# Two layers of a streaming encoder on one core: recurrent gates as 64x128 blocks, their heads and the local attention heads in alternating row halves of the array

## The chip, the cores and the metric

The kernel runs on one core of one Trainium2 chip. The metric is the device time of one execution in microseconds (us), as the median of several runs. Engine names are those of the profile: PE is the matrix engine (TensorE), PEld its weight loads, DVE the vector engine, ACT the scalar engine, SP the engine that issues the loads of weights. A matmul multiplies a stationary operand, which a weight load brings into the 128x128 array, with a moving operand of N columns, and writes to PSUM.

## The reference

Two layers run over a sequence of 256 positions with 1024 features, in float32. Only the parts of the mixer that the change touches are shown; before and after the mixer each layer has a gated feed-forward block (width 2816).

```python
# recurrent branch: 16 heads of 64 features, two gates per head
xb = xc.reshape(B, S, LRU_BLOCKS, LRU_BLOCK)                 # 16 blocks of 64
r  = sigmoid(einsum('bshi,hij->bshj', xb, wa) + ba)
gi = sigmoid(einsum('bshi,hij->bshj', xb, wx) + bx)
log_a = -LRU_C * r * softplus(-lam);  a = exp(log_a)
b = sqrt(max(1 - exp(2 * log_a), 0)) * gi * xc               # then a scan over time
# local attention: 8 query heads and 2 key/value heads of 64, window of 3 chunks of 64
s = einsum('bcqkgd,bcskd->bckgqs', qb, kb) * 64 ** -0.5 - slopes * dist
p = softmax over keys, with a learned sink per head
o = einsum('bckgqs,bcskd->bcqkgd', p, vb)
```

A third branch is attention over 256 memory tokens. The three branches are projected, gated, summed and projected again.

## The kernel before, in words

Activations are kept feature-major: 128 features on the partitions, 256 positions along the free dimension, eight such chunks for 1024 features. Every weight is cut on the host into blocks of 128x128, in the order in which the kernel uses them, eight blocks to a slab of 128x1024 numbers. SP loads slabs; ACT rounds each to a high half (`whi`, line 194) and DVE subtracts to get the low half (`wlo`, line 195). A product is formed with reduced-precision matmuls: high weight times both halves of the activations (512 columns, line 219) and low weight times the high half (256 columns, line 220).

The order of the work is written out by hand. `block` hands out the next weight block; at the first block of each slab it prepares the slab that is three ahead and calls `tick`, which runs the side tasks that are due. `at(n, f)` makes f due n ticks later, so a tick comes once per 8 blocks, just before the matmuls of the next slab. What is issued so goes into the in-order queues of PE, ACT and DVE.

In `mix` (one call per layer) the stretch that matters runs as follows.

- `conv` projects the recurrent input and runs a convolution on ACT and DVE; its result is split into halves `xcs`.
- Then come the projections of keys and values (`pkv`), and four pairs of query projections (`pq`, `pq`, `pcq`, `pcq`), each of 16 blocks. After each of the four pairs stands `lru_gates(p)`: two gates times two chunks, each gate of a chunk being one 128x128 block with two 64x64 heads on its diagonal and zeros elsewhere, and three matmuls of 256 columns per block (lines 670 to 672, tile `lg`). Four sigmoids of 128x256 on ACT take them out of PSUM (lines 675 and 676), and DVE multiplies `gi` with the convolution (line 677).
- `decay(c)` puts three ACT functions (`e`, `nth`, `a`, lines 706 to 708) and one DVE operation (`ms`, line 709) per chunk on the ticks behind that, under the projections `pyr` and `pgt`. `e` and `nth` take turns in a pool of three buffers, so that `nth` of a chunk waits for `ms` of the chunk before.
- `attention_tasks` spreads the two attentions over the same ticks. For query tile qt (0 or 1) and key/value head g (0 or 1), `win_scores` runs four matmuls over 64 partitions (line 835, tile `ws`, the upper 64 partitions for g = 1), DVE adds the distance (line 837), `win_max`, `win_exp` and `win_norm` (line 861) make probabilities `P`, and `win_transpose` turns them on PE (line 877, tile `wt`) and has ACT copy them (line 878, `PT`). For qt = 1 the scores of a g are split over two ticks.

Two PSUM pools matter. `mm` has three tiles of two banks, used by all projections and by `lg`; `att` has two tiles of one bank, used in turn by `ws`, `wt` and the memory attention's `ms`. A full-precision matmul, as in `ws`, `wt` and `wv`, is recorded as two passes, transposes as one. `win_values` (lines 888 and 890, tile `wv`) writes g = 0 and g = 1 to different halves of the array's columns, one after the other.

`join` takes a projection out of PSUM: ACT copies one half, and one tick later DVE adds the other (line 261), which frees the `mm` tile; line 635 then multiplies with the norm.

Of the kernel before, what the change touches and what calls it, by code (L numbers as in the profile page):

```python
# [22 lines left out]
AF = mybir.ActivationFunctionType  # L23
ALU = mybir.AluOpType
# [10 lines left out]
HB = 8  # L35
EPS = 1e-6
BIG = 1e30
NBLK = 2 * 1728
NSLAB = NBLK // HB
WIN_SCALE = 0.125  # L40
MEM_SCALE = 128.0 ** -0.5
# [29 lines left out]
def cols(c):  # L71
    return slice(c, c + 128)
# [22 lines left out]
class Trunk:  # L95
# [46 lines left out]
    def mm(self, nm):  # L142
        return self.pmm.tile([128, 2, 2, 256], F32, tag="mm", name=self.name(nm))
# [481 lines left out]
    def mix(self, l, norm, nxt):  # L625
        nc, V, A, G = self.nc, self.nc.vector, self.nc.scalar, self.nc.gpsimd
        w = lambda base, p: (lambda m: [("w_in", l, cols(128 * k), cols(base + 128 * (2 * p + m))) for k in range(KT)])
# [4 lines left out]
        xcs = Halves(self, "xcs")  # L632
# [28 lines left out]
        gi, r = self.big("gi"), self.big("r")  # L661

        def lru_gates(p):
            ps = self.mm("lg")
            for i, nm in enumerate(("lru_wa", "lru_wx")):
                for m in range(2):
                    c = 2 * p + m
                    hi, lo = self.block(nm, l, None, ("bd", c))
                    mm = nc.tensor.matmul
                    mm(ps[:, i, m, :], hi, xcs.hi(c), start=True, stop=False)  # L670
                    mm(ps[:, i, m, :], hi, xcs.lo(c), start=False, stop=False)
                    mm(ps[:, i, m, :], lo, xcs.hi(c), start=False, stop=True)
            for m in range(2):
                c = 2 * p + m
                A.activation(r[:, c, :], ps[:, 0, m, :], AF.Sigmoid, bias=self.vec("lru_ba", l, c))
                A.activation(gi[:, c, :], ps[:, 1, m, :], AF.Sigmoid, bias=self.vec("lru_bx", l, c))
            V.tensor_tensor(gi[:, sl(p), :], gi[:, sl(p), :], xc[:, sl(p), :], op=ALU.mult)

        kv = self.ps2.tile([128, 2, 256], F32, tag="kv", name=self.name("kv"), bufs=1)
        ps = self.pair("pkv", w(C_K, 0), norm.xs)  # L680
# [10 lines left out]
        qcq = self.big("qcq")  # L691
        for p in range(4):
            if p < 2:
                ps = self.pair("pq", lambda m: [("w_in", l, cols(128 * k), ("q", 2 * p + m)) for k in range(KT)], norm.xs)
            else:
                ps = self.pair("pcq", w(C_CQ, p - 2), norm.xs)
            project(qcq[:, sl(p), :], ps)
            lru_gates(p)


        a, ms = self.big("a"), self.big("ms")
# [51 lines left out]
        for p in range(4):  # L753
            ps = self.pair("pyr", w(C_YR, p), norm.xs)
# [11 lines left out]
        for g in range(3):  # L766
            gt = self.big(f"g{g}")
            gates.append(gt)
            for p in range(4):
                ps = self.pair("pgt", w(C_G + 1024 * g, p), norm.xs)  # L770
# [32 lines left out]
        n = self.Norm(self, *nxt)  # L803
# [16 lines left out]
    def attention_tasks(self, l, kv, vt, qcq, out):  # L820
        nc, V, A, T, G = self.nc, self.nc.vector, self.nc.scalar, self.nc.tensor, self.nc.gpsimd
        k = kv[:, 0, :]
        sinks = self.vec("attn_sinks", l)
        st = {}

        def win_scores(qt, g, js):
            n = 128 * (qt + 1)
            qs = slice(128 * qt, 128 * qt + 128)
            gp = slice(64 * g, 64 * g + 64)
            P = self.h4("P") if js[0] == 0 else st["w", qt, g]  # L830
            st["w", qt, g] = P
            d = self.dist[:, 0:128] if qt == 0 else self.dist[:, 128:384]
            ps = self.att("ws").rearrange("p (a n) -> p a n", n=n)
            for j in js:
                T.matmul(ps[:, j - js[0], :], qcq[gp, j, qs], k[gp, 0:n], start=True, stop=True)
            for j in js:
                V.scalar_tensor_tensor(P[:, j, 0:n], d, -8.0 * 2.0 ** -(4 * g + j + 1), ps[:, j - js[0], :],
                                       op0=ALU.mult, op1=ALU.add)

        def win_max(qt, g):  # L840
            n = 128 * (qt + 1)
            P = st["w", qt, g]
            mx, ng, es, den = (self.sm(s) for s in ("mx", "ng", "es", "den"))
            sk = sinks[:, 4 * g:4 * g + 4]
            V.tensor_reduce(mx, P[:, :, 0:n], axis=AX.X, op=ALU.max)
            V.scalar_tensor_tensor(mx, mx, WIN_SCALE, sk, op0=ALU.mult, op1=ALU.max)
            V.tensor_scalar(ng, mx, -1.0, None, op0=ALU.mult)
            V.tensor_tensor(es, sk, mx, op=ALU.subtract)
            st["w", qt, g] = (P, ng, es, den)

        def win_exp(qt, g):
            n = 128 * (qt + 1)
            P, ng, es, den = st["w", qt, g]
            for j in range(4):
# [80 lines left out]
                             start=(t == 0), stop=(t == 1))  # L935
            self.split(ps, out["C"], 0, 4, delay=0)

        for (qt, g), ts in (((0, 0), (1, 3, 4, 7)), ((0, 1), (3, 5, 6, 9)), ((1, 0), (10, 12, 13, 15)),
                            ((1, 1), (13, 15, 16, 18))):
            for i in range(qt + 1):  # L940
                self.at(ts[0] + i, win_scores, qt, g, range(2 * i, 2 * i + 2) if qt else range(4))
            self.at(ts[0] + qt, win_max, qt, g)
            for t, f in zip(ts[1:], (win_exp, win_norm, win_transpose)):
                self.at(t, f, qt, g)
        for qt, ts in enumerate(((16, 17, 19, 22), (19, 20, 22, 24))):
# [6 lines left out]
    def run(self):  # L952
        nc = self.nc
        n = self.start()
        for l in range(DEPTH):
# [14 lines left out]
            if not last:  # L970
                n.then(5, 7)
        assert len(self.order) == NBLK

# [4 lines left out]
def pack_weights(order, inp):  # L978
    out = np.zeros((NSLAB, 128, HB, 128), np.float32)
    for i, (w, l, rows, cls) in enumerate(order):  # L980
        dst = out[i // HB, :, i % HB, :]
        if rows is None:
            c = cls[1]
            dst[0:64, 0:64] = inp[w][l, 2 * c]
            dst[64:128, 64:128] = inp[w][l, 2 * c + 1]
            continue
        if isinstance(rows, tuple):
            rows = QROWS[rows[1]]
        if isinstance(cls, tuple):
            cls = QROWS[cls[1]]  # L990
        dst[...] = inp[w][l][rows, cls]
    return out.reshape(NSLAB, 128, HB * 128)


def pack_vectors(inp):
    pk = np.zeros((128, NVEC), np.float32)
    for (v, l), o in VOFF.items():
        if v == "final_norm":
            a = inp[v].reshape(8, 128).T
        elif v == "attn_sinks":  # L1000
            a = np.broadcast_to(inp[v][l], (128, 8))
        else:
            a = inp[v][l].reshape(-1, 128).T
        pk[:, o:o + a.shape[1]] = a
    return pk

# [38 lines left out]
```

## Time and profile before

| | |
|---|---|
| median of 3 runs (1285.68 to 1287.1) | 1286.26 us |
| the profiled execution's own time | 1286.29 us |
| its span, first to last instruction | 1284.3 us |
| PE busy | 1269.7 us (99%) |
| PE weight loads busy | 1116.4 us (87%) |
| DVE busy | 980.7 us (76%) |
| ACT busy | 758.8 us (59%) |
| TensorE clock granted, mean share of full | 0.997 |

The profile has a page (busy times, the chain of work that ended last, the costliest groups) and a trace that can be asked for timelines and sums over stretches. A timeline line gives start, length, engine, source line, operation, the tile written and the tiles read, and in brackets the idle time before it and who ended it. Matmuls are pipelined, so their lengths overlap: what a matmul costs is the distance between starts.

### The profile page before, as it was taken

How to read it: one execution, taken by the hardware profiler on the slowest of the kernel's cores; microseconds unless marked ns; L12 is line 12 of the kernel's file. 1: busy time of each engine (PE TensorE's matmuls, PEld its weight loads, DVE VectorE, ACT ScalarE, POOL GpSimd, SP SyncE). 2: the span in 40 equal slices, each digit the busy share in tenths (PEclk: the TensorE clock that was granted, in tenths of full speed). 3: DMA queues.
4: the chain of work that ended last, by engine and by line, in shares of the span. 5: the costliest groups of instructions: out<-in, count | busy, mean ns of one | idle time of the engine just before them, and what ended most of it. 6: DMA issues, size and time to landing. Idle time of an engine off the chain costs nothing.

```text
span 1284.3 us, 19477 instructions
## 1 busy us (share of the span) xinstructions
PE 1269.7 (99%) x7514; PEld 1116.4 (87%) x7514; DVE 980.7 (76%) x1398; ACT 758.8 (59%) x1129; POOL 0.3 (0%) x5
## 2 busy tenths in 40 slices
PE   9999999999999999999999999999999999999997
PEld 7888898888888888888988888988888889888886
DVE  8788766888789887666668775669887898776754
ACT  6656544587578555554456564447857675655542
POOL 0000000000000000000000000000000000000000
PEclk9999999999999999999999999999999999999998
DMA  8665655555446555566556656555554465665651
GB/s 295 212 183 167 212 192 168 178 178 166 133 131 199 194 180 189 191 193 198 185 192 204 193 183 195 185 185 155 181 164 132 153 197 176 197 192 187 196 183 47
DMA packets 64748, 232.42 MB, mean 181 GB/s; under 512 B 7312, under 2 KB 7440, under 8 KB 64400
## 3 DMA queue, kind: packets, MB, share of 16 engines
q1 hardware_dynamic: 64224, 230.65, 56.3%
q8 instruction: 59, 0.97, 0.3%
q10 hardware_dynamic: 432, 0.53, 0.1%
q14 instruction: 33, 0.27, 0.1%
HBM read 230.10 MB, written 1.05 MB: 180 GB/s over the span
## 4 chain that ended last, share of the span: by engine, by line
PE 90%; DVE 5%; ACT 2%; issue 1%; DMA 1%; SPq 0%; DVEq 0%; ACTq 0%
PE pg L219 11%; PE pu L219 11%; PE pd L219 9%; PE pgt L219 6%; PE pu L220 6%; PE pg L220 6%; PE pd L220 5%; PE pbr L219 4%; PE pgt L220 3%; DVE wlo L195 2%; PE pyr L219 2%; PE pbr L220 2%; PE pxr L219 2%; PE pwo L219 2%; PE pgu L219 2%; PE pd L238 2%
## 5 line engine op out<-in xcount | busy, mean ns | idle before, releaser
L195 DVE TENSOR_TENSOR wlo<-st,whi 128x1024 fp32r<-128x1024 f32 (+2 forms) x438 | 524.6, 1206 | 252.9 <-ACT whi L194 252.8
L194 ACT ACTIVATE whi<-st 128x1024 fp32r<-128x1024 f32 (+2 forms) x438 | 444.1, 1045 | 35.9 <-PE pd L219 20.5
L219 PE MATMUL pg<-xs,whi 128*128 128x512 f32 x640 | 225.4, 394 | 0.0
L219 PE MATMUL pu<-xs,whi 128*128 128x512 f32 x640 | 225.2, 394 | 0.0
L219 PE MATMUL pd<-h,whi 128*128 128x512 f32 x528 | 184.1, 393 | 0.0
L220 PE MATMUL pg<-xs,wlo 128*128 128x256 f32 x640 | 179.4, 280 | 0.0
L220 PE MATMUL pu<-xs,wlo 128*128 128x256 f32 x640 | 179.3, 280 | 0.0
L220 PE MATMUL pd<-h,wlo 128*128 128x256 f32 x528 | 148.0, 280 | 0.0
L219 PEld LDWEIGHTS pg<-xs,whi 128*128 128x128 f32 x640 | 119.9, 187 | 27.2
L219 PEld LDWEIGHTS pu<-xs,whi 128*128 128x128 f32 x640 | 119.8, 187 | 27.0
L219 PE MATMUL pgt<-xs,whi 128*128 128x512 f32 x384 | 139.1, 405 | 0.0
L220 PEld LDWEIGHTS pu<-xs,wlo 128*128 128x128 f32 x640 | 121.0, 189 | 0.0
L220 PEld LDWEIGHTS pg<-xs,wlo 128*128 128x128 f32 x640 | 121.0, 189 | 0.0
L219 PEld LDWEIGHTS pd<-h,whi 128*128 128x128 f32 x528 | 98.9, 187 | 22.5
L220 PE MATMUL pgt<-xs,wlo 128*128 128x256 f32 x384 | 107.5, 280 | 0.0
L220 PEld LDWEIGHTS pd<-h,wlo 128*128 128x128 f32 x528 | 99.8, 189 | 0.0
L219 PEld LDWEIGHTS pgt<-xs,whi 128*128 128x128 f32 x384 | 72.1, 188 | 19.5 <-issue 3.0
L258 ACT COPY g<-pg 128x512 f32<-128x512 f32 x40 | 23.5, 586 | 100.5 <-PE pg L220 93.3
L220 PEld LDWEIGHTS pgt<-xs,wlo 128*128 128x128 f32 x384 | 72.5, 189 | 0.2
L270 ACT ACTIVATE h<-u 128x512 fp32r<-128x512 f32 x44 | 27.8, 632 | 46.0 <-DVE u L523 43.8
L320 ACT ACTIVATE xs<-x,pk 128x256 fp32r<-128x256 f32 x40 | 18.7, 504 | 60.8 <-DVE x L557 21.6
L238 PE MATMUL pd<-h,wlo 128*128 128x256 f32 x176 | 49.8, 283 | 0.0
(246 smaller groups left out, 2259.0 us busy)
## 6 DMA issues: line engine op xcount, KB each, us to landing
st<-wpack SPq DMA_DIRECT2D x428, 512.0 KB, 3.8
st<-wpack SPq DMA_DIRECT2D x8, 256.0 KB, 5.3
mem<-memT SPq DMA_DIRECT2D x2, 1024.0 KB, 6.5
x<-xT SPq DMA_DIRECT2D x4, 256.0 KB, 5.4
outT<-xg SPq DMA_DIRECT2D x2, 256.0 KB, 2.6
outT<-xg ACTq DMA_DIRECT2D x2, 256.0 KB, 2.8
cst<-cst SPq DMA_DIRECT2D x1, 320.0 KB, 6.1
pk<-pk SPq DMA_DIRECT2D x1, 128.0 KB, 5.8
```

Source lines behind the costliest of these rows:

```text
L194: nc.scalar.activation(hi[:, c], st[:, c], AF.Copy)
L195: nc.vector.tensor_tensor(lo[:, c], st[:, c], hi[:, c].bitcast(F32), op=ALU.subtract)
L219: mm(both, hi, X.both(k), start=(k == 0), stop=False)
L220: mm(out[:, 0, :], lo, X.hi(k), start=False, stop=(k == n - 1))
L238: mm(out, lo, X.hi(k), start=False, stop=(k == len(blocks) - 1))
L258: self.nc.scalar.copy(dst, ps[:, :, 1, :])
L270: hi = lambda: self.nc.scalar.activation(X.hi(k, n), src, AF.Copy)
L320: self.t.nc.scalar.activation(self.xs.hi(k), x[:, k, :], AF.Copy, scale=self.t.vec(self.v, self.l, k))
```

## The change

The gates' weights are packed without zeros. For chunk c with heads 2c and 2c+1 one block now holds in its upper 64 rows the two gates' 64x64 matrices of head 2c side by side, and in its lower 64 rows those of head 2c+1 in swapped order. A matmul takes 64 rows of the block and of the activations and writes 128 columns: both gates of one head. So a chunk needs one block where it needed two, and still six matmuls of 256 columns, now alternating between the upper and the lower rows. The two heads go to the two banks of the `lg` tile. Each sigmoid covers 64 partitions, and there are eight per pair of chunks instead of four. The biases of the second gate are stored with their halves swapped.

The scores of the local attention are taken for both g in one task, into both `att` tiles, with matmuls alternating between g = 0 and g = 1. For qt = 0 that is one task at tick 1 (before: ticks 1 and 3), for qt = 1 two tasks at ticks 10 and 11 (before: 10, 11, 13 and 14). The number of slabs falls by one per layer.

```diff
-NBLK = 2 * 1728
+NBLK = 2 * 1720
...
-            for i, nm in enumerate(("lru_wa", "lru_wx")):
-                for m in range(2):
-                    c = 2 * p + m
-                    hi, lo = self.block(nm, l, None, ("bd", c))
-                    mm = nc.tensor.matmul
-                    mm(ps[:, i, m, :], hi, xcs.hi(c), start=True, stop=False)
-                    mm(ps[:, i, m, :], hi, xcs.lo(c), start=False, stop=False)
-                    mm(ps[:, i, m, :], lo, xcs.hi(c), start=False, stop=True)
+            mm = nc.tensor.matmul
+            halves = (slice(0, 64), slice(64, 128))
             for m in range(2):
                 c = 2 * p + m
-                A.activation(r[:, c, :], ps[:, 0, m, :], AF.Sigmoid, bias=self.vec("lru_ba", l, c))
-                A.activation(gi[:, c, :], ps[:, 1, m, :], AF.Sigmoid, bias=self.vec("lru_bx", l, c))
+                hi, lo = self.block("lru_w", l, None, ("bd", c))
+                for i, (w, x) in enumerate(((hi, xcs.hi(c)), (hi, xcs.lo(c)), (lo, xcs.hi(c)))):
+                    for j, q in enumerate(halves):
+                        mm(ps[:, j, m, :], w[q, :], x[q, :], start=(i == 0), stop=(i == 2))
+            for m in range(2):
+                c = 2 * p + m
+                for j, q in enumerate(halves):
+                    A.activation(r[q, c, :], ps[q, j, m, :], AF.Sigmoid, bias=self.vec("lru_ba", l, c)[q, :])
+                    o = halves[1 - j]
+                    A.activation(gi[q, c, :], ps[o, j, m, :], AF.Sigmoid, bias=self.vec("lru_bx", l, c)[o, :])
...
+            ps = [self.att("ws").rearrange("p (a n) -> p a n", n=n) for _ in range(2)]
             for j in js:
-                T.matmul(ps[:, j - js[0], :], qcq[gp, j, qs], k[gp, 0:n], start=True, stop=True)
-            for j in js:
-                V.scalar_tensor_tensor(P[:, j, 0:n], d, -8.0 * 2.0 ** -(4 * g + j + 1), ps[:, j - js[0], :],
-                                       op0=ALU.mult, op1=ALU.add)
+                for g in range(2):
+                    gp = slice(64 * g, 64 * g + 64)
+                    T.matmul(ps[g][:, j - js[0], :], qcq[gp, j, qs], k[gp, 0:n], start=True, stop=True)
+            for g in range(2):
+                P = self.h4("P") if js[0] == 0 else st["w", qt, g]
+                st["w", qt, g] = P
+                for j in js:
+                    V.scalar_tensor_tensor(P[:, j, 0:n], d, -8.0 * 2.0 ** -(4 * g + j + 1), ps[g][:, j - js[0], :],
+                                           op0=ALU.mult, op1=ALU.add)
...
-        for (qt, g), ts in (((0, 0), (1, 3, 4, 7)), ((0, 1), (3, 5, 6, 9)), ((1, 0), (10, 12, 13, 15)),
+        self.at(1, win_scores, 0, range(4))
+        for i in range(2):
+            self.at(10 + i, win_scores, 1, range(2 * i, 2 * i + 2))
+        for (qt, g), ts in (((0, 0), (1, 3, 4, 7)), ((0, 1), (3, 5, 6, 9)), ((1, 0), (11, 12, 13, 15)),
                             ((1, 1), (13, 15, 16, 18))):
-            for i in range(qt + 1):
-                self.at(ts[0] + i, win_scores, qt, g, range(2 * i, 2 * i + 2) if qt else range(4))
-            self.at(ts[0] + qt, win_max, qt, g)
+            self.at(ts[0], win_max, qt, g)
```

How instructions stand on PE where the last group of gates meets the first scores, in layer 0 (names end in buffer numbers; `xcs` are the convolution's halves, `kv` and `qcq` keys and queries). Before:

```order
L670 MATMUL lg_2753<-xcs_2207,whi_2660 128x256
L671 MATMUL lg_2753<-xcs_2207,whi_2660 128x256
L672 MATMUL lg_2753<-xcs_2207,wlo_2661 128x256
L835 MATMUL ws_2784<-kv_2414,qcq_2474 128x128 x4
L219 MATMUL pyr_2774<-xs_1420,whi_2684 128x512 [waits DVE_49]
```

With the change:

```order
L672 MATMUL lg_2759<-xcs_2207,whi_2652 128x256 x4
L672 MATMUL lg_2759<-xcs_2207,wlo_2653 128x256 x2
L836 MATMUL ws_2793<-kv_2414,qcq_2474 128x128
L836 MATMUL ws_2794<-kv_2414,qcq_2474 128x128
L836 MATMUL ws_2793<-kv_2414,qcq_2474 128x128
L836 MATMUL ws_2794<-kv_2414,qcq_2474 128x128
L836 MATMUL ws_2793<-kv_2414,qcq_2474 128x128 [waits DVE_49]
L836 MATMUL ws_2794<-kv_2414,qcq_2474 128x128
L836 MATMUL ws_2793<-kv_2414,qcq_2474 128x128
L836 MATMUL ws_2794<-kv_2414,qcq_2474 128x128
L219 MATMUL pyr_2784<-xs_1420,whi_2676 128x512 [waits DVE_49]
```

The scores of both g now stand directly behind the gates, and the second visit, 16 blocks later, is gone.

On PE at tick 10, in the projection `pgt`, before:

```order
L220 MATMUL pgt_3077<-xs_1421,wlo_2978 128x256
L835 MATMUL ws_3115<-kv_2414,qcq_2474 128x256 [waits Activation_49]
L835 MATMUL ws_3115<-kv_2414,qcq_2474 128x256
L219 MATMUL pgt_3077<-xs_1420,whi_3010 128x512
L220 MATMUL pgt_3077<-xs_1420,wlo_3011 128x256 [waits DVE_49]
```

With the change:

```order
L220 MATMUL pgt_3087<-xs_1421,wlo_2988 128x256
L836 MATMUL ws_3124<-kv_2414,qcq_2474 128x256 [waits Activation_49]
L836 MATMUL ws_3125<-kv_2414,qcq_2474 128x256 [waits Activation_49]
L836 MATMUL ws_3124<-kv_2414,qcq_2474 128x256
L836 MATMUL ws_3125<-kv_2414,qcq_2474 128x256
L219 MATMUL pgt_3087<-xs_1420,whi_3020 128x512
L220 MATMUL pgt_3087<-xs_1420,wlo_3021 128x256 [waits DVE_49]
```

The visit now takes two `att` tiles where it took one, and each has its own wait for ACT.

On DVE behind the last gates, before:

```order
L837 SCALAR_TENSOR_TENSOR P_2783<-cst,ws_2784 128x128 [waits PE_49]
L837 SCALAR_TENSOR_TENSOR P_2783<-cst,ws_2784 128x128 x3
L845 TENSOR_REDUCE mx_2793<-P_2783 128x4 [waits DVE_49]
L846 SCALAR_TENSOR_TENSOR mx_2793<-mx_2793,pk 128x4 [waits DVE_49]
L847 TENSOR_SCALAR ng_2794<-mx_2793 128x4 [waits DVE_49]
L848 TENSOR_TENSOR es_2795<-pk,mx_2793 128x4
L709 SCALAR_TENSOR_TENSOR ms_2772<-e_351_2801,nth_2802 128x256 [waits Activation_49]
L195 TENSOR_TENSOR wlo_2826<-st_2682,whi_2825 128x1024 [waits DMAHW6_49,Activation_49]
L709 SCALAR_TENSOR_TENSOR ms_2772<-e_353_2829,nth_2830 128x256 [waits Activation_49]
L195 TENSOR_TENSOR wlo_2856<-st_2716,whi_2855 128x1024 [waits DMAHW7_49,PE_49,Activation_49]
L837 SCALAR_TENSOR_TENSOR P_2864<-cst,ws_2865 128x128 [waits PE_49]
L837 SCALAR_TENSOR_TENSOR P_2864<-cst,ws_2865 128x128 x3
```

With the change:

```order
L841 SCALAR_TENSOR_TENSOR P_2803<-cst,ws_2793 128x128 [waits PE_49]
L841 SCALAR_TENSOR_TENSOR P_2803<-cst,ws_2793 128x128 x3
L841 SCALAR_TENSOR_TENSOR P_2808<-cst,ws_2794 128x128 [waits PE_49]
L841 SCALAR_TENSOR_TENSOR P_2808<-cst,ws_2794 128x128 x3
L849 TENSOR_REDUCE mx_2813<-P_2803 128x4 [waits DVE_49]
L850 SCALAR_TENSOR_TENSOR mx_2813<-mx_2813,pk 128x4 [waits DVE_49]
L851 TENSOR_SCALAR ng_2814<-mx_2813 128x4 [waits DVE_49]
L852 TENSOR_TENSOR es_2815<-pk,mx_2813 128x4
L711 SCALAR_TENSOR_TENSOR ms_2782<-e_350_2821,nth_2822 128x256 [waits Activation_49]
```

The four operations of the second tile stand ahead of the first `ms`, the DVE part of `decay`, where they stood behind the second.

## Rows read from the trace of the kernel before

**Rows 1.** Page, busy time: us (share of the span) and instructions.
```profile
PE 1269.7 (99%) x7514; PEld 1116.4 (87%) x7514; DVE 980.7 (76%) x1398; ACT 758.8 (59%) x1129; POOL 0.3 (0%) x5
```
**Rows 2.** Page, the chain of work that ended last, by engine.
```profile
PE 90%; DVE 5%; ACT 2%; issue 1%; DMA 1%; SPq 0%; DVEq 0%; ACTq 0%
```
**Rows 3.** Sum over one stretch for tile lg: window, length, PE, PEld, ACT busy.
```profile
269.20:270.70 1.50, 1.45 (x12) 1.45 (x12) 0.00 (x0) 1.00 0.93 273
```
**Rows 4.** Timeline of PE, tick 10: start us, length us, engine, line.
```profile
306.25 0.28 PE L220 MATMUL pgt<-xs,wlo 128*128 128x256 f32 x1
306.45 1.13 PE L835 MATMUL ws<-kv,qcq 64*128 64x256 f32 x4
...
307.85 0.28 PE L220 MATMUL pgt<-xs,wlo 128*128 128x256 f32 x1
```
**Rows 5.** Timeline of PE, last gates, first scores and the projection behind them.
```profile
277.67 0.28 PE L672 MATMUL lg<-xcs,wlo 128*128 128x256 f32 x1
277.88 1.16 PE L835 MATMUL ws<-kv,qcq 64*128 64x128 f32 x8
...
279.30 0.28 PE L220 MATMUL pyr<-xs,wlo 128*128 128x256 f32 x1
```
**Rows 6.** Timeline of PE around the attention values, in column halves.
```profile
345.35 0.65 PE L888 MATMUL wv<-PT,vt 128*64 128x256 f32 x4
...
348.43 0.28 PE L220 MATMUL pgt<-xs,wlo 128*128 128x256 f32 x1
```
**Rows 7.** Timeline of DVE and PE behind the first group of gates.
```profile
255.48 0.68 DVE L261 TENSOR_TENSOR kv<-pkv,kv 128x512 f32<-128x512 f32 x1
...
256.31 0.47 PE L219 MATMUL pq<-xs,whi 128*128 128x512 f32 x1 [0.75 <-ACT xcs L270]
```
**Rows 8.** Timeline of ACT, last sigmoid of the second group.
```profile
266.01 0.50 ACT L676 ACTIVATE gi<-lg,pk 128x256 f32<-128x256 f32 x1
266.37 2.04 ACT L194 ACTIVATE whi<-st 128x1024 fp32r<-128x1024 f32 x2
```
**Rows 9.** Timeline of DVE behind the second group.
```profile
267.35 0.68 DVE L677 TENSOR_TENSOR gi<-gi,xc 128x512 f32<-128x512 f32 x1
...
269.08 0.68 DVE L261 TENSOR_TENSOR qcq<-pq,qcq 128x512 f32<-128x512 f32 x1
```
**Rows 10.** Timeline of ACT, first sigmoid of the fourth group to the second transposes' copy.
```profile
277.99 0.47 ACT L675 ACTIVATE r<-lg,pk 128x256 f32<-128x256 f32 x1 [0.84 <-PE lg L672]
...
285.44 0.51 ACT L707 ACTIVATE nth<-r,lc 128x256 f32<-128x256 f32 x1 [0.96 <-DVE ms L709]
...
305.76 0.57 ACT L878 COPY PT<-wt 128x512 f32<-128x512 f32 x1
```
**Rows 11.** Sum over a stretch: window, length, PE, PEld, DVE, ACT busy.
```profile
285.40:307.30 21.90, 21.90 (x130) 18.96 (x128) 20.55 (x39) 21.85 (x52) 0.00 (x0) 1.00 0.51 159
```
**Rows 12.** Timeline of DVE: scores taken from PSUM, and probabilities made.
```profile
283.01 0.88 DVE L837 SCALAR_TENSOR_TENSOR P<-cst,ws 128x128 f32<-128x128 f32 x4
...
294.12 0.69 DVE L861 TENSOR_TENSOR P<-P,den 128x512 f32<-128x512 f32 x1
...
300.13 0.69 DVE L861 TENSOR_TENSOR P<-P,den 128x512 f32<-128x512 f32 x1
...
309.66 0.75 DVE L837 SCALAR_TENSOR_TENSOR P<-cst,ws 128x256 f32<-128x256 f32 x2
...
320.93 1.23 DVE L861 TENSOR_TENSOR P<-P,den 128x1024 f32<-128x1024 f32 x1
```
**Rows 13.** Timeline of PE: transposes, and the second visit of qt = 1.
```profile
297.10 0.60 PE L877 MATMUL wt<-cst,P 128*128 128x128 f32 x4
...
303.11 0.60 PE L877 MATMUL wt<-cst,P 128*128 128x128 f32 x4
...
310.49 1.13 PE L835 MATMUL ws<-kv,qcq 64*128 64x256 f32 x4
...
325.32 1.33 PE L877 MATMUL wt<-cst,P 128*128 128x128 f32 x8
```

More of the change, by code (lines that the diff above doesn't have):

```diff
@@ L824, in attention_tasks, with win_scores @@
         st = {}
-        def win_scores(qt, g, js):
+        def win_scores(qt, js):
             n = 128 * (qt + 1)
             qs = slice(128 * qt, 128 * qt + 128)
-            gp = slice(64 * g, 64 * g + 64)
-            P = self.h4("P") if js[0] == 0 else st["w", qt, g]
-            st["w", qt, g] = P
             d = self.dist[:, 0:128] if qt == 0 else self.dist[:, 128:384]
-            ps = self.att("ws").rearrange("p (a n) -> p a n", n=n)
+            ps = [self.att("ws").rearrange("p (a n) -> p a n", n=n) for _ in range(2)]
             for j in js:
-                T.matmul(ps[:, j - js[0], :], qcq[gp, j, qs], k[gp, 0:n], start=True, stop=True)
-            for j in js:
-                V.scalar_tensor_tensor(P[:, j, 0:n], d, -8.0 * 2.0 ** -(4 * g + j + 1), ps[:, j - js[0], :],
-                                       op0=ALU.mult, op1=ALU.add)
+                for g in range(2):
[7 more added lines that the diff above has]
+                                           op0=ALU.mult, op1=ALU.add)
         def win_max(qt, g):
@@ L983, in pack_weights @@
             c = cls[1]
-            dst[0:64, 0:64] = inp[w][l, 2 * c]
-            dst[64:128, 64:128] = inp[w][l, 2 * c + 1]
+            wa, wx = inp["lru_wa"][l], inp["lru_wx"][l]
+            dst[0:64] = np.concatenate([wa[2 * c], wx[2 * c]], axis=1)
+            dst[64:128] = np.concatenate([wx[2 * c + 1], wa[2 * c + 1]], axis=1)
             continue
@@ L1003, in pack_vectors @@
             a = inp[v][l].reshape(-1, 128).T
+        if v == "lru_bx":
+            a = np.concatenate([a[64:], a[:64]])
         pk[:, o:o + a.shape[1]] = a
```

## The prediction

> **What bounds the kernel now.** The busy times come first: PE is busy for 99% of the span [rows 1]. The chain of work that ended last gives PE 90% of it [rows 2]. So a microsecond that PE no longer needs is a microsecond of the time, as long as nobody makes PE wait instead. That condition is the question here, because the stretch that the change touches is the one place in a layer where others are nearly full too: over 21.9 us from the first `decay` to the second transposes, ACT is busy for 21.85 and DVE for 20.55 [rows 11]. The start of PE's query projection waits 0.75 us for a PSUM tile that a DVE operation frees [rows 7]. Such lines tell where PE time is worth something and where it isn't. I walk through layer 0; layer 1 has the same instructions, and I count it twice. "Late" and "early" are against the trace of before.
>
> **Prices.** (1) A full gate matmul of 256 columns: 12 take 1.45 us [rows 3], so 0.12 each and 1.44 a group. (2) A visit to matmuls over 64 rows. Between the starts at 306.25 and 307.85 lie 1.60 us [rows 4]. Of that 0.12 is the first matmul, 0.24 the 512 columns behind the visit (two of 256), and the four passes of 256 columns cost 0.216 each, 0.86 together (1.13 for four of which the last is seen at full length). What is left, 0.38, is paid for going to 64 rows and back, about half each way. The visit for qt = 0 gives the same: 1.63 [rows 5], less 0.36, less eight passes of 0.112, is 0.37. So a visit costs 1.25 or 1.27.
>
> (3) What the trace does not show is two halves of rows at work at once. The dearest case is that they follow each other: 0.12 each, no gain. The cheapest is a pair in the time of one. The nearest row is the attention values, in halves of columns [rows 6]: 32 passes, half of 256 columns and half of 128. One after the other they would need 16 x 0.216 + 16 x 0.11 = 5.2 us. From 345.35 to 348.43 there are 3.1, of which 0.24 are the 512 columns behind them and about 0.3 the loads and the switch back: 2.6, half. I take pairs in the time of one: 0.72 for a group of gates.
>
> (4) A sigmoid over 64 partitions. The trace has it over 128 partitions, 0.36 from start to start [rows 8]: 266.01 to 266.37. At least it could cost half, if time went with partitions; at most 0.36 each. Each lane still has 256 numbers to go through, so I take 0.36: four more are 1.44 us of ACT per group, 5.8 a layer, less one `whi` of 1.0.
>
> **On paper** PE gains a lot. Six visits a layer before (two for qt = 0, four for qt = 1); six with the change (four groups of gates, the last together with the scores for qt = 0, and two for qt = 1). So no switch is added, 2.9 us of gates, 0.9 and 1.7 us of scores go away: 5.5 a layer.
>
> **What is left of it,** place by place:
>
> - *First gates.* PE stands waiting behind them until DVE has freed a tile at 255.48 + 0.68 [rows 7]. Gain: none.
> - *Second gates.* PE 0.34 early. ACT ends their eight sigmoids 1.6 late (1.44, and 0.16 left over from the first group), so `gi` on DVE, at 267.35 in the row, starts at about 268.15, and the `whi` behind the sigmoids comes 1.6 late too, so that its `wlo` starts at 269.07. Behind it stands the addition that frees the tile of the fourth query pair, at 269.08 in the row [rows 8, 9]: now 270.2 to 270.9. PE would be there at 270.1, starts at 271.1, and started at 270.70, at the end of the group's window [rows 3]: **0.4 late**. The third group's gain is lost here.
> - *Fourth gates and first scores.* Less 0.72, plus 0.2 for the switch in: the gates end 0.1 early, the scores and switch out leave PE 0.3 early. ACT starts the sigmoids at 277.9 and ends them 1.34 late. DVE reaches the scores as much late, and takes eight operations instead of four (0.88 [rows 12], so 0.8 more) before `ms`. ACT waits for `ms` even now [rows 10]: it goes on at 287.55 instead of 285.44, **2.1 late**. From there to the copy of the second transposes it has no idle time to give [rows 11], so that copy ends at 308.45 instead of 306.33.
> - *Transposes for qt = 0.* One visit less: PE 1.6 early, at 295.5. But the probabilities, made at 294.12 [rows 12], come 1.45 late (DVE follows ACT's `nth`, and has its four operations less), at 296.25. PE goes on 0.7 early [rows 13]. The second transposes want the probabilities of 300.13, now 1.85 late, done at 302.67: PE 0.25 early.
> - *Tick 10.* PE comes at 306.2 instead of 306.45 [rows 4]. It needs two tiles now, and the second is freed by the copy that ends at 308.45. So the visit ends at 309.6 instead of 307.6: **2.0 late**.
> - *Tick 11.* PE comes at 312.3 (310.49 + 2.0, less 0.2 for the switch [rows 13]). It needs both tiles back from DVE: 309.66 in the row, now 1.95 late behind a `wlo` that waits for ACT, and four operations of 0.34: the second tile is free at 313.05. The visit ends at 314.25, where it ended at 311.64 (310.49 + 1.13, and the pass's tail instead of the way back): **2.6 late**.
> - *Ticks 13 and 14.* Two visits of 1.25 are gone: **0.1 late**.
>
> The transposes behind that find their probabilities ready: DVE, 2.45 late by the walk, ends them at 324.6 instead of 322.16 [rows 12], and PE is due at 325.4 [rows 13]. So nothing more is lost. The removed slab costs nothing on PE: its blocks' matmuls are counted above, and its load, `whi` and `wlo` were off the path. Sum: 0.1 x 2 = 0.2 late on the profiled execution's 1286.29 (0.03 above the median shown): **1286.4 us**. Five microseconds a layer would be removed from PE and given back as waits for PSUM tiles.
>
> The Trainium skill has the rule that fits this: TensorEngine Tiling (Array Packing), section PSUM Bottleneck, says that tiling speeds up the matrix engine but not the emptying of PSUM, which may then bind. By that rule the walk above, and not the sum on paper, decides.
>
> **Rivals.**
>
> *The gain survives.* If neither ACT nor DVE kept PE waiting, all but the first group's 0.7 and a little would stay: 5.2 a layer, 1276. For it: PE's 90% of the chain. Against it: ACT's and DVE's busy times in just this stretch [rows 11]. Chance 0.07.
>
> *Sigmoids at half price.* With the lower bound of price (4) ACT has no more work than before. The fourth query pair then starts 0.6 early, the fourth gates let ACT go 1.1 early, the eight operations on DVE bring ACT to 0.35 early at the copy: 306.0. PE arrives at tick 10 at 303.9, still waits 2, leaves 0.5 early, leaves tick 11 0.3 late, and gains 2.5: 2.2 a layer, **1282**. With other small errors of the same sign, between 1280 and 1283.7: chance 0.20.
>
> *The halves take turns.* This is the one that ends slower. Place: each group of gates and each pair of scores. If a half waits for the other, a group costs 1.44 + 0.38 instead of 1.44. PE is 0.8 late at the fourth gates, 1.7 behind the scores; ACT is 3.2 late at the copy (309.55), the visit of tick 10 with eight passes in turn ends 3.5 late, that of tick 11 4.4, and 2.5 come back: 1.9 a layer, **1290**. It decides as soon as a pair costs 0.06 more than a single one, for then the groups cost what they did. For it: no row shows two row halves at once. Against it: the column halves do overlap, weight loads included [rows 6]. Chance 0.18, and 0.08 for other ways to be slower by more than 0.2%, a further wait behind tick 11 above all.
>
> The Trainium skill has a rule that speaks for this rival: TensorE: Matmul & The Clock Gate, section LDWEIGHTS, says that a load's time goes with the columns and not with the rows, at columns / 1.2 ns. Twelve loads in series would by that be an estimated 1.28 us a group, more than the pairs' 0.72, and the time would be near the rival's 1290; no run here shows whether loads of two row halves overlap.
>
> **How the numbers follow.** The forecast, between 1283.7 and 1288.8, has 0.47: within 0.2% (2.6 us, about what a measurement of this kernel can tell from no change) counts as the same. Faster: 0.07 + 0.20 = 0.27. Slower: 0.18 + 0.08 = 0.26. The range goes from 1281, which holds most of the half-price case, to 1290.5, which takes in the turns.
>
> **What would show it.** In the changed profile: `lg` starts in pairs a few ns apart, 0.12 from pair to pair, 0.2 lost before and behind a group; eight sigmoids 0.36 apart; PE waiting before the fourth query pair (0.9), before the first transposes (0.8), at tick 10 for ACT's copy (2.2) and at tick 11 for DVE (0.6); no `ws` at ticks 13 and 14. The forecast is wrong if sigmoids over 64 partitions are clearly cheaper, if the copy at tick 10 ends before 307, or if row halves start 0.12 apart.

## The result, and the profile after

The changed kernel took 1294.76 us (median of 5 runs, 1293.12 to 1295.52) against 1286.65 for the kernel before on the same occasion: ratio 1.0059, 95% interval 1.0047 to 1.0071. It is 8 us slower; the forecast was 1286.4 and the range ended at 1290.5.

The page of the profiled execution (1293.75 us, span 1292.0), busy times and the chain that ended last:

```profile
PE 1265.3 (98%) x7514; PEld 1111.0 (86%) x7514; DVE 979.3 (76%) x1396; ACT 775.2 (60%) x1159; POOL 0.3 (0%) x5
...
PE 85%; ACT 8%; DVE 5%; issue 1%; DMA 0%; DVEq 0%; ACTq 0%
```

PE is busy 4.4 us less than before [rows 1] and yet the end is later. ACT is busy 16.4 us more, and has gone from 2% to 8% of the chain [rows 2]. So PE has less work, and loses more than that by waiting. Where, the idle times of PE in layer 0 tell (waiter, tile, line, releaser: us in all, times, longest):

```profile
PE pcq L219 <- DVE qcq L261: 2.0, 1, 2.0
PE ws L836 <- ACT PT L882: 1.6, 1, 1.6
PE wt L881 <- ACT whi L194: 1.4, 1, 1.4
PE pq L219 <- ACT xcs L270: 1.3, 1, 1.3
PE lg L672 <- ACT gi L678: 0.8, 2, 0.5
PE wt L881 <- ACT P L914: 0.3, 1, 0.3
```

Together these are 7.4 us. The kernel before has 0.75 of them, before the second query pair [rows 7], and 0.2 at a transposes' tile. The list puts the wait before the second query pair down to ACT's `xcs`, but PE's weight load there began at 254.77, just before `xcs` ended and 0.12 behind DVE's addition, so the addition is the likelier releaser. The list holds idle time of PE's matmuls only; a load that waits while a matmul is still recorded as running is not in it (tick 11, below). The weight loads and matmuls of the first group of gates:

```profile
252.53 0.30 PEld L672 LDWEIGHTS lg<-xcs,whi 64*128 64x128 f32 x4 [0.26 <-issue]
252.76 0.19 PEld L672 LDWEIGHTS lg<-xcs,wlo 64*128 64x128 f32 x2
252.88 0.30 PEld L672 LDWEIGHTS lg<-xcs,whi 64*128 64x128 f32 x4
253.12 0.19 PEld L672 LDWEIGHTS lg<-xcs,wlo 64*128 64x128 f32 x2
```

Three pairs start between 252.53 and 252.88, 0.12 a pair. Four loads of 0.185 each are done in 0.30, so the two row halves load at once. That part is as forecast. Now ACT at the second group, eight sigmoids and the `whi` behind them:

```profile
264.56 0.47 ACT L676 ACTIVATE r<-lg,pk 64x256 f32<-64x256 f32 x1
265.04 0.47 ACT L678 ACTIVATE gi<-lg,pk 64x256 f32<-64x256 f32 x1
265.53 0.47 ACT L676 ACTIVATE r<-lg,pk 64x256 f32<-64x256 f32 x1
...
267.46 0.47 ACT L676 ACTIVATE r<-lg,pk 64x256 f32<-64x256 f32 x1
267.94 0.47 ACT L678 ACTIVATE gi<-lg,pk 64x256 f32<-64x256 f32 x1
268.43 2.00 ACT L194 ACTIVATE whi<-st 128x1024 fp32r<-128x1024 f32 x2
```

Each lasts 0.47, as over 128 partitions. But the next starts 0.48 behind and not 0.36 [rows 8]: the overlap of 0.12 between neighbours is gone. A group takes 3.87 from its first sigmoid to the `whi`, where it took 1.44: 2.4 more, and the forecast had 1.44 more. DVE and PE behind it:

```profile
268.44 0.69 DVE L679 TENSOR_TENSOR gi<-gi,xc 128x512 f32<-128x512 f32 x1 [2.39 <-ACT gi L678]
269.53 1.23 DVE L195 TENSOR_TENSOR wlo<-st,whi 128x1024 fp32r<-128x1024 f32 x1 [0.39 <-ACT whi L194]
270.67 0.68 DVE L261 TENSOR_TENSOR qcq<-pq,qcq 128x512 f32<-128x512 f32 x1
```

```profile
269.16 0.28 PE L672 MATMUL lg<-xcs,wlo 64*128 64x256 f32 x2
271.41 0.50 PE L219 MATMUL pcq<-xs,whi 128*128 128x512 f32 x1 [1.97 <-DVE qcq L261]
```

DVE, which ran through here without a gap [rows 9], stands 2.39 for the sigmoids, and the addition that frees PE's tile is last in its queue. The stretches behind that wait (window, length, PE, PEld, DVE, ACT, POOL busy, granted clock, the transfers' share and GB/s):

```profile
270.00:272.00 2.00, 0.59 (x3) 0.55 (x4) 1.97 (x4) 1.98 (x5) 0.00 (x0) 1.00 0.07 4
272.00:276.00 4.00, 4.00 (x16) 3.43 (x15) 2.14 (x4) 3.91 (x8) 0.00 (x0) 0.58 0.75 253
276.00:280.00 4.00, 4.00 (x36) 3.46 (x37) 3.42 (x4) 1.50 (x3) 0.00 (x0) 1.00 0.42 140
```

After the idle time the granted clock falls to the lower level (1.2 GHz, shown as 0.58 for a stretch that is partly at 2.4) for some 3.4 us. In the kernel before the mixer runs at 1.00 throughout. Further on, ACT at its wait for `ms` and at the copy of the second transposes, and PE at ticks 10 and 11 and at the transposes for qt = 1:

```profile
290.31 0.51 ACT L709 ACTIVATE nth<-r,lc 128x256 f32<-128x256 f32 x1 [1.63 <-DVE ms L711]
...
310.62 0.58 ACT L882 COPY PT<-wt 128x512 f32<-128x512 f32 x1
```

```profile
308.96 0.70 PE L836 MATMUL ws<-kv,qcq 64*128 64x256 f32 x2
311.25 1.13 PE L836 MATMUL ws<-kv,qcq 64*128 64x256 f32 x6 [1.60 <-ACT PT L882]
315.33 1.63 PE L836 MATMUL ws<-kv,qcq 64*128 64x256 f32 x8
315.83 0.73 PEld L836 LDWEIGHTS ws<-kv,qcq 64*128 64x128 f32 x6 [0.21 <-DVE P L841]
328.09 1.04 PE L881 MATMUL wt<-cst,P 128*128 128x128 f32 x8
```

At tick 11 the loads for the second tile wait for DVE: from its first matmul to the projection's next one the visit takes 1.56, where a visit took 1.06 before.

The program runs 1.51 ahead at the second query pair (254.80 against 256.31 [rows 7]), which comes from the stages ahead of the mixer and was not looked into. With that taken off, `nth` is 6.4 late against [rows 10] and so is the copy; PE ends tick 11 at 316.96, 6.9 late against [rows 13], and the transposes 4.3.

### The profile page after: what moved, and what is told of

Same layout as the page of the kernel before. It is cut to its first block, busy times and chain, and to the rows that moved or that the text cites. A ratio compares the mean times of both kernels' runs of the same rounds, so it can differ in the third digit from the quotient of the medians.

```text
span 1292.0 us, 19505 instructions
## 1 busy us (share of the span) xinstructions
PE 1265.3 (98%) x7514; PEld 1111.0 (86%) x7514; DVE 979.3 (76%) x1396; ACT 775.2 (60%) x1159; POOL 0.3 (0%) x5
## 4 chain that ended last, share of the span: by engine, by line
PE 85%; ACT 8%; DVE 5%; issue 1%; DMA 0%; DVEq 0%; ACTq 0%
PE pg L219 11%; PE pu L219 11%; PE pd L219 9%; PE pgt L219 6%; PE pg L220 6%; PE pu L220 6%; PE pd L220 5%; PE pbr L219 4%; PE pgt L220 3%; PE pgu L219 2%; ACT whi L194 2%; DVE wlo L195 2%; PE pbr L220 2%; PE pwo L219 2%; PE pxr L219 2%; PE pd L238 2%
```

## The experiments

Each was timed 4 to 11 times, beside the kernel before. The table collects, for layer 0, how late three places are against the kernel before, counted in each trace from the start of the mixer's first projection (`pxr`): the first weight load of the fourth group of gates, the end of ACT's copy of the second transposes, and the mixer's end (start of `pbr`), this also for layer 1.

| kernel | gates 4 | copy | end, layer 0 | end, layer 1 | ratio (95%) |
|---|---|---|---|---|---|
| the change | +4.0 | +6.4 | +4.2 | +4.3 | 1.0059 (1.0047 to 1.0071) |
| gates only | +3.9 | +5.6 | +5.0 | +3.7 | 1.0067 (1.0055 to 1.0080) |
| attention only | 0.0 | +0.7 | -1.4 | -1.4 | 0.9983 (0.9974 to 0.9992) |
| wide sigmoids | -0.5 | -0.5 | -2.6 | -2.6 | 0.9960 (0.9947 to 0.9972) |
| sigmoids in another order | +3.1 | +4.9 | +2.9 | +1.4 | 1.0037 (1.0023 to 1.0051) |
| before, sigmoids split | +2.5 | +5.0 | +4.4 | +4.4 | 1.0069 (1.0055 to 1.0082) |
| wait filled | +2.5 | +4.9 | +4.3 | +4.2 | 1.0065 (1.0052 to 1.0077) |
| both waits filled | +2.4 | +4.8 | +3.8 | +3.9 | 1.0054 (1.0040 to 1.0067) |
| attention only, later | +0.1 | +0.7 | -1.5 | -1.7 | 0.9975 (0.9966 to 0.9985) |
| attention only, spread | 0.0 | +0.7 | -3.4 | -3.3 | 0.9943 (0.9931 to 0.9956) |
| spread, gates, other order | +1.6 | +3.4 | -0.7 | +0.8 | 1.0008 (0.9999 to 1.0017) |
| spread, gates, wide sigmoids | -0.5 | -0.5 | -4.6 | -4.6 | 0.9921 (0.9908 to 0.9935) |

**The two parts apart.** First the gates of the change with the attention of before.

> The gates in row halves as in the change, the attention as before. In the changed kernel's trace PE waits 1.97 us for the tile of the fourth query pair, behind sigmoids that start 0.48 us apart (0.36 over 128 partitions), and then runs for 3.6 us at half the clock; from the third group of gates on it is 4.0 us a layer later than before, and 4.2 at the end of the mixer. Theory (the sigmoids over 64 partitions cost the time): it is all still there, 8 sigmoids 0.48 apart, the wait of about 2 us and the half clock, and the time is 1293 to 1297, since the attention's part of the change is near nothing. Rival (the scores of both g in one task cost the time): the time falls to 1288 or less.

1295.09 us. Then the attention of the change with the gates of before.

> The attention in pairs of halves as in the change, the gates as before (4 sigmoids over 128 partitions a group). Theory (the sigmoids cost the time): no wait before the fourth query pair and full clock behind it; PE saves 1.3 us a layer at the first visit and 2.5 at ticks 13 and 14, waits some 1.6 at tick 10 for the copy of the second transposes and 0.5 at tick 11: 1.0 to 2.0 a layer saved, 1282.5 to 1284.7. Rival (the scores of both g in one task cost the time): 1290 or more.

1284.2 us; PE's only new idle time is the one at tick 10, and at tick 11 the loads wait for DVE, as in the changed kernel:

```profile
PE ws L834 <- ACT PT L880: 0.9, 1, 0.9
```

```profile
312.37 0.73 PEld L834 LDWEIGHTS ws<-kv,qcq 64*128 64x128 f32 x6 [0.25 <-DVE P L839]
```

The loss is all in the gates. The attention's part by itself gains 2.3 us.

**Wide sigmoids.**

```diff
-                for j, q in enumerate(halves):
-                    A.activation(r[q, c, :], ps[q, j, m, :], AF.Sigmoid, ...)
-                    o = halves[1 - j]
-                    A.activation(gi[q, c, :], ps[o, j, m, :], AF.Sigmoid, ...)
+                A.activation(r[:, c, :], ps[:, 0, m, :], AF.Sigmoid, ...)
+                A.activation(gi[:, c, :], ps[:, 1, m, :], AF.Sigmoid, ...)
```

> The changed kernel with 4 sigmoids over 128 partitions a group in place of 8 over 64: the second head of each chunk gets its two gates exchanged, which leaves the output other than the reference's; every other instruction is the changed kernel's. Theory (the sigmoids cost the time): sigmoids 0.36 apart, PE's wait before the fourth query pair below 0.5 us, full clock, and a time below that of before: 1279 to 1284. Rival (PE's row halves cost it, by their switches and loads): the groups of gates in the trace stay as long, and the time stays above 1290. Rival (the paired scores cost it): the wait is gone, the time still 1288 or more.

1281.29 us. With nothing changed but ACT's sigmoids the wait, the low clock and all of the loss are gone, and PE's halves gain. ACT at the second group, 0.36 apart:

```profile
266.16 0.50 ACT L675 ACTIVATE r<-lg,pk 128x256 f32<-128x256 f32 x1
266.52 0.51 ACT L676 ACTIVATE gi<-lg,pk 128x256 f32<-128x256 f32 x1
266.88 1.10 ACT L194 ACTIVATE whi<-st 128x1024 fp32r<-128x1024 f32 x1
```

**The sigmoids in another order** (the edit is shown in short, `r of j, m` standing for the sigmoid that writes `r` of half j and chunk m).

```diff
-            for m in range(2):
-                for j, q in enumerate(halves):
-                    (r of j, m), (gi of j, m)
+            for j, q in enumerate(halves):
+                (r of j, m = 0), (r of j, m = 1), (gi of j, m = 0), (gi of j, m = 1)
```

> The changed kernel with the 8 sigmoids of a group in another order: first both chunks for one gate and half, then for the next, so that 4 of the 7 neighbours read and write the same partitions as the one before. If the 0.12 us of overlap is lost because the range of partitions changes between neighbours, 4 of 7 distances fall to 0.36, a group's sigmoids end 0.5 earlier and the time falls to 1291 to 1293. If it is lost because an operation covers 64 partitions only, all distances stay 0.48 and the time stays within 1 us of the changed kernel's 1294.8.

1290.78 us, just below the first range. ACT at the first group (x2: two in a row):

```profile
259.60 0.83 ACT L677 ACTIVATE r<-lg,pk 64x256 f32<-64x256 f32 x2
260.44 0.83 ACT L680 ACTIVATE gi<-lg,pk 64x256 f32<-64x256 f32 x2
261.29 0.83 ACT L677 ACTIVATE r<-lg,pk 64x256 f32<-64x256 f32 x2
262.13 0.83 ACT L680 ACTIVATE gi<-lg,pk 64x256 f32<-64x256 f32 x2
```

Two on the same partitions take 0.83 together, so they start 0.36 apart; the next, on another half, starts behind their end (0.84). So not the 64 partitions cost the overlap, but that a neighbour reads or writes another half. A group takes 3.39 from its first sigmoid to the `whi` (259.60 to 262.99) in place of 3.87, and the time is 4.0 lower, some of it because the low clock comes in one layer only. Eight sigmoids that are all 0.36 apart were not tried.

This run also shows what the low clock costs, for both layers have the same wait and only the first the low clock. PE at the fourth query pair in layer 0 and 1, and the 6.0 us behind each:

```profile
272.51 0.50 PE L219 MATMUL pcq<-xs,whi 128*128 128x512 f32 x1 [1.76 <-DVE qcq L261]
...
905.89 0.50 PE L219 MATMUL pcq<-xs,whi 128*128 128x512 f32 x1 [1.77 <-DVE qcq L261]
```

```profile
272.50:278.50 6.00, 5.99 (x25) 5.18 (x26) 4.59 (x6) 4.74 (x9) 0.00 (x0) 0.72 0.54 176
905.90:911.90 6.00, 6.00 (x34) 5.04 (x36) 4.58 (x6) 4.78 (x10) 0.00 (x0) 1.00 0.53 176
```

The layers end 2.9 and 1.4 late (table): 1.5 for the clock. The run of the gates only has it in layer 0 alone, too, behind waits of 1.97 in both layers: 5.0 and 3.7.

**Filling the wait.**

```diff
+            if p == 2:
+                for _ in range(2):
+                    w8 = self.att("warm")
+                    for _ in range(4):
+                        mm(w8, hi, xcs.both(c), start=True, stop=True)
```

> The changed kernel with 8 matmuls of 512 columns more behind the third group of gates, into the two attention tiles, read by nobody: PE multiplies where it waited 1.97 us for the tile of the fourth query pair. ACT, DVE and the moment at which that tile is free stay as they are. Theory (the wait costs twice, by itself and by the half clock behind it): the clock stays at 1.00 from 270 to 278 us, the fourth query pair takes 5.7 us where it took 7.3, and the time falls by about 1.6 a layer, to 1291 to 1292.5. Rival (the clock falls for another reason, or what it costs is hidden by ACT, which is late anyway): the time stays within 1 us of the changed kernel's 1294.8.

1294.62 us, which looks like the rival. But the windows show something else:

```profile
272.00:276.00 4.00, 4.00 (x21) 3.14 (x20) 3.47 (x4) 3.92 (x9) 0.00 (x0) 1.00 0.38 129
...
312.00:316.00 4.00, 3.98 (x13) 2.95 (x14) 3.96 (x7) 0.92 (x1) 0.00 (x0) 0.57 0.67 237
```

The clock holds behind the first wait, and falls behind that of tick 10 instead, in both layers. That wait is 1.60 us, as in the changed kernel, where the clock stayed at 1.00 behind it. So the cost was moved, and the time can't tell. Then both waits were filled, the second with four matmuls into the `ws` tile ahead of the scores:

> The kernel with the filled wait, and at tick 10 four full-precision matmuls of 512 columns more into the first attention tile, ahead of the scores that overwrite it. In the run before, filling the first wait kept the clock at 1.00 there (the fourth query pair took 5.6 us in place of 7.3), but the half clock came at tick 10 instead, for some 3 us behind a wait of 1.60, and the time stayed. Theory (the half clock was moved, not removed, and costs about 1 us a layer wherever it falls): no stretch of the mixer below 0.95 of the clock, and 1291.5 to 1293.3. Rival (ACT's lateness alone sets the time, whatever PE's clock): full clock and still 1294 to 1295.5. If the four matmuls last longer than the wait at tick 10 (1.6 us) they cost by themselves; the trace shows it.

1294.33 us at full clock throughout the mixer. PE at tick 10:

```profile
308.78 3.59 PE L840 MATMUL ws<-cst 128*128 128x512 f32 x8
312.31 0.92 PE L845 MATMUL ws<-kv,qcq 64*128 64x256 f32 x6
```

The filling lasted 3.59 us, and ended 1.2 behind the copy that the scores wait for (at 311.12 in this trace, by the table's +4.8). So it gave back about what the clock would have cost. As a whole-program time this run settles nothing; the pairs of layers above do.

**The sigmoids alone.** The kernel before, with each sigmoid cut in two:

```diff
-                A.activation(r[:, c, :], ps[:, 0, m, :], AF.Sigmoid, ...)
-                A.activation(gi[:, c, :], ps[:, 1, m, :], AF.Sigmoid, ...)
+                for i, (t, b) in enumerate(((r, "lru_ba"), (gi, "lru_bx"))):
+                    for q in (slice(0, 64), slice(64, 128)):
+                        A.activation(t[q, c, :], ps[q, i, m, :], AF.Sigmoid, ...)
```

> The kernel before with one thing changed: each sigmoid over 128 partitions is two over 64, lower and upper, so that a group has 8 and neighbours never work on the same partitions. PE's work, the weights and the attention are those of before. Theory (the 8 sigmoids and what they set off cost the time, PE's halves nothing): sigmoids 0.48 apart, a wait of 1 to 2 us before the fourth query pair with half the clock behind it, 1291 to 1297. Rival (the row halves on PE, with their switches, are needed for the loss): below 1289.

1294.98 us: PE's halves aren't needed for the loss, nor is the low clock, which this mixer doesn't have. Here PE waits at three places, for two PSUM pools:

```profile
PE wt L878 <- ACT PT L879: 1.7, 1, 1.7
PE pcq L219 <- DVE qcq L261: 1.3, 1, 1.3
...
PE lg L670 <- ACT gi L677: 0.5, 1, 0.5
```

**The attention made to pay.** Next, the attention alone with the visits of qt = 1 one tick later.

```diff
-            self.at(10 + i, win_scores, 1, range(2 * i, 2 * i + 2))
+            self.at(11 + i, win_scores, 1, range(2 * i, 2 * i + 2))
-((1, 0), (11, 12, 13, 15))
+((1, 0), (12, 13, 14, 16))
```

> The attention's part of the change alone, with the two visits of the second query tile at ticks 11 and 12 in place of 10 and 11, and what follows for its g = 0 one tick later. In the run of the attention alone PE waits 0.88 us at tick 10 for the copy of the second transposes and leaves that visit 1.6 late of what it came with. Theory (that wait is where the tile is asked for before ACT has emptied it): no wait at tick 11, 2.5 us a layer below before, 1280.5 to 1282.5. Rival (a new wait in place of the old one, behind the later probabilities of g = 0 at ticks 14 to 16): 1283.5 or more.

1283.52 us, as the rival has it: the wait is gone at the scores and back at the memory scores, which now share a tick with the transposes (the first row below). So these were moved apart, too:

```diff
-((1, 1), (13, 15, 16, 18))
+((1, 1), (13, 15, 16, 19))
-((16, 17, 19, 22), (19, 20, 22, 24))
+((17, 18, 20, 22), (20, 21, 22, 24))
-        self.at(20, win_values)
+        self.at(21, win_values)
```

> The attention alone, its second query tile at ticks 11 and 12, and the memory attention's first scores one tick later than the transposes that share their tiles (17 in place of 16, what follows moved with them, the last transposes of the local attention at 19, its values at 21). In the run of the attention later PE waited 1.1 us a layer at the memory scores, for ACT to empty a transposes' tile asked for in the same tick. Theory (PSUM tiles asked for before ACT can have emptied them are what is left between this kernel and its gain on PE): that wait goes, 1280.5 to 1282.5. Rival (a new wait further back, at the values or the last transposes): 1283 or more.

1279.83 us, 7.1 below before, below the theory's range and faster than both kernels. PE's idle time in layer 0: of the version before this the row that was to go, and all of this one:

```profile
PE ms L903 <- ACT PT L880: 1.1, 1, 1.1
```

```profile
PE pq L219 <- ACT xcs L270: 0.8, 1, 0.8
PE wt L879 <- DVE P L863: 0.3, 1, 0.3
```

**The gates on top of that.**

> The changed kernel with its sigmoids in the better order (neighbours 0.37 or 0.48 apart) and the attention's ticks of the spread version, which alone took 1279.8. What PE saves in the gates is some 1.4 us a layer, what the 8 sigmoids add on ACT is some 1.9 a group. Theory (ACT is the bound from the first gates on, and its lateness reaches PE through whichever PSUM tile comes next): the gates lose 3 to 5 us on the spread version: 1282.5 to 1285. Rival (the loss in the changed kernel came from the ticks 10 and 11 that the paired scores share with ACT's copies, and is gone with them): 1280 or less.

1286.7 us, no different from the kernel before, and some 7 above the spread version without them (6.8 by the two layers of the table): slower than the theory's range, and far from the rival's. One layer had the low clock, the other not (0.8 and -0.7 in the table).

> The same with 4 sigmoids over 128 partitions a group in place of 8, which exchanges the two gates of every second head and leaves the output other than the reference's. It shows what the gates in row halves are worth on PE when ACT does no more than before. Theory: 1.4 us a layer below the spread version, 1276 to 1278. Rival (another bound is reached, DVE's tiles or the convolution before the gates): 1279 to 1280.

1275.3 us. With ACT's work as before, PE's row halves are worth 1.2 us a layer (-3.4 to -4.6), and the gates, the paired scores and the moved ticks together take 10 us off the kernel before (1285.55 on this occasion). With two gates exchanged this is a price, not a kernel to use.

## Why the prediction was wrong

**The step that failed is price (4).** "At most 0.36 each", the upper bound, was no bound: it took the start-to-start distance of sigmoids over 128 partitions for a property of the operation. It is 0.47 of work less 0.12 of overlap with a neighbour on the same partitions, and the overlap was the part that the change takes away. The guess that time doesn't go with partitions was right (0.47 either way). Measured, four more sigmoids cost 2.4 us of ACT a group, not 1.44.

**Second gates.** The walk named the right chain: sigmoids, `gi`, `whi`, `wlo`, the addition, PE's tile. With 2.4 in place of 1.44 in each of two groups ACT left the second group's sigmoids 3.6 late (268.43 + 1.51 against 266.37), where the walk had 1.6, and PE was 2.2 late there (271.41 + 1.51 against the 270.70 of [rows 3]), not 0.4. The first group did harm, too: its sigmoids held the tile of the second, and PE waited 0.5.

**What the walk put at nothing** is the clock. Behind the longer wait, 1.97 instead of the 0.9 that it gave PE, the clock fell in both layers, and with the wait filled it held there. That cost 1.5 us a layer where the layers of one run can be compared. The wait's length alone does not explain the fall (last section).

**The eight operations on DVE** ahead of `ms` were right: forecast 0.8, and 0.7 late at the copy with the attention alone.

**The copy at tick 10** was 6.4 late, not 2.1. Put into the walk, the dearer sigmoids add 1.8 at the fourth query pair (2.2 for 0.4) and 1.0 at the fourth group: an estimated 4.9, and the two kernels with the wait filled, whose clock held up to there, show 4.9 and 4.8. The clock adds 1.5: 6.4. At the end of the mixer the same sum is 0.1 + 2.8 (1.8 and 1.0) + 1.5 = 4.4 a layer, and 4.2 and 4.3 were measured. In the walk ACT had no idle time to win it back [rows 11], which held: `nth` and the copy are equally late.

**Ticks 10, 11, 13 and 14** went as said, on top of that lateness. At tick 10 PE came at 308.96 and had the second tile at 311.25, 2.3 later (forecast 2.2; 1.6 of it idle), and left 6.3 late. At tick 11 the wait for DVE came, some 0.5 (forecast 0.6), and PE left 6.9 late. Without the two later visits it was 2.5 better off: 4.3 (forecast 2.6 and 0.1).

**The prices on PE** were right: pairs at 0.12, no gain at the first group, and the rival that they take turns is out. Its time, 1290, was on the right side for the wrong reason. The rule of the Trainium skill, TensorE: Matmul & The Clock Gate, section LDWEIGHTS, that a load's time goes with its columns and not its rows, gave an estimated 1.28 us for a group's loads in series. The trace agrees on the rows (0.19 for a load of 64 rows as for one of 128); that the loads go in series was the prediction's own addition, and they don't: they are done in pairs from 252.53 to 253.31. What TensorEngine Tiling (Array Packing), section PSUM Bottleneck, says, that tiling doesn't speed up the emptying of PSUM, the trace bears out, with more than that: emptying got dearer, 3.87 us for 1.44.

**The half-price rival** was worked out at 1282 for an ACT with no more work than before. The kernel with wide sigmoids is that case, and took 1281.3, with PE 0.7 early at the fourth query pair (worked out: 0.6), the copy 0.5 early (0.35) and 2.6 a layer gained (2.2). So at these places the walk held to 0.4, once ACT's work was what it had assumed.

## What to carry to other kernels

A distance between starts belongs to a pair of neighbours, not to one operation: before cutting operations up, ask what their overlap rests on, and put the full length of one (here 0.47, not 0.36) as the upper end. When tiling an engine that is 99% busy makes another engine's emptying dearer, count that engine's queue up to the last tile that the first one needs; here the gates' row halves paid only where the reader kept its number of operations and its partitions. Moving tasks to other ticks, which had looked like a detail, was worth more here (2.0 us a layer between the first and the last attention version) than the matmuls' packing (1.2).

## What the runs showed of the hardware

- ACT starts an operation some 0.12 us ahead of the end of the one before it where both work on the same 64 partitions or both on all 128, and not where input or output change halves (0.36 against 0.48). In the changed kernel `gi` and the `r` behind it differ in the output's half alone, `r` and the `gi` behind it in input and bias alone, and both pairs are 0.48 apart (264.56, 265.04, 265.53): either is enough. The step from 128 partitions to the lower 64 keeps it: a copy that starts at 264.09 and lasts 0.58 is followed at 264.56. Input and bias were not tried apart.
- A wait of PE of 1.76 and 1.77 us, at the same place of two equal layers, was followed by the lower clock once and by the full one once; so was one of 1.97 in the run of the gates only. Behind waits of 1.60 it fell in one kernel and held in another, behind 1.3 it held. What decides, besides the wait's length, stays open.
- Loads and matmuls of the two row halves of the array overlap fully: a pair of 64 rows costs 0.12, as one of 128 rows does (252.53 to 252.88 for three pairs).
